# Weight-block sums loaded through a third buffer, low parts moved between DMA and VectorE, and two down slabs carried by the up stream

## The chip, the cores and the metric

The kernel runs on one NeuronCore of a Trainium2 chip. Inside a core, TensorE (PE) multiplies matrices, VectorE (DVE) and ScalarE (ACT) do elementwise work, GpSimd (POOL) and SyncE (SP) issue DMAs here. The metric is the device time of one execution in microseconds; less is better.

## The reference

One encoder layer on a sequence of 512 positions with 1024 channels, in float32. Only its last part is touched by the change, a gated feed-forward net:

```python
FFN_DIM = 3072
...
        h = rmsnorm(x, ffn_pre_norm[l])
        up = causal_dwconv(h @ w_ffn_up[l], ffn_conv_w[l], ffn_conv_b[l])
        f_gate, f_val = jnp.split(up, 2, axis=-1)
        f = (jax.nn.gelu(f_gate, approximate=True) * f_val) @ w_ffn_down[l]
        x = x + rmsnorm(f, ffn_post_norm[l])
```

Ahead of it stand a Mamba-2 mixer, a gated recurrent mixer and their merge; they take the first 480 us of the execution and are the same before and after.

## The kernel before

**Precision.** Every float32 operand is split into two parts, `hi` (the value in the matmul's reduced format) and `lo` (the rest). A product is three matmuls: hi by hi, hi by lo, lo by hi. The hi part is a copy on ACT, the lo part a subtraction `src - hi`, on DVE by `tensor_sub`, or in two places by DMA: ACT writes `-hi` into `lo` and a DMA issued from POOL with `accum_op=add` adds the source to it.

**Up stage.** The up matrix is cut into 24 pairs n = 0 to 23 of slabs, a gate slab and a value slab of 128 output channels. Pairs 0 to 3 (`PLAIN`) use the general slab stream. From n = 4 the pairs repeat as two "seven" pairs and one "eight" pair (6, 9, 12, 15, 18, 21 are eights, called plain pairs below). An eight makes its 2x2 block product in full: four stretches of 12 matmuls of 512 columns, weights a11, a12 (gate), then a21, a22 (value). A seven computes the same by seven block products of 12 matmuls of 256 columns (Strassen's scheme in Winograd's form), in the order a11, s2, s4, s3, a12, s1, and a22 as the "last product", which is issued during the next pair. The s blocks are sums of weight blocks: s1 = a21 + a22, s3 = a11 + a21, s2 = s1 + a11, s4 = s2 + a12 (the value half comes out with its sign turned, which its convolution weights `negw` undo). The matching sums of the activations, `tsum`, are made once; `h_split` splits them into `comb`.

**Where the blocks come from.** `pair_load(n)` brings the two slabs of a pair (1024 KB) into one of two slots of the tile `ring` (shown as H), issued by SP two pairs ahead. `pair_sums(n)` makes s1 and s3 by DMA: SP loads the first block (256 KB) into a buffer, then POOL adds the second block from memory with an accumulating DMA. Buffers: `place("raw", n % 2)` for s1, `2 + n % 2` for s3. s2 (line 953) and s4 (line 956) are DVE additions. `w_split(g)` splits block g of the stream, five blocks ahead of its use, into a ring of six half tiles of `whi` and `wlo`. In an eight, a11 and a12 are split in one go of 1024 columns, and so are a21 and a22; for the second of these the low part goes by DMA (line 973).

**What sets the order.** PE, ACT and, up to line 297, DVE keep the program's order. From there on DVE, and SP and POOL throughout, run in the order that a scheduler chooses at build time. Each queue is then strictly in order, so an instruction that waits holds up all behind it.

**What waits for what in a seven.** `block_product` of a12 adds to the same PSUM bank that line 1021 reads (`u2`), and the last product adds to the bank that lines 1035 and 1036 read (the sums with `u4`). So PE waits for DVE there. The pair slot is free once all its blocks are split.

**Down stage.** After pair 23 the down matrix comes as 24 slabs through the general stream. Before the change the first two are loaded in slot 1 of pair 23 and split in slot 4 of pair 23 and during the first down turn, into the tile `first` (H).

Of the kernel before, what the change touches and what calls it, by code (L numbers as in the profile page):

```python
# [8 lines left out]
F32 = mybir.dt.float32  # L9
# [5 lines left out]
P = 128  # L15
D = 1024
# [40 lines left out]
def block_kernel(ctx: ExitStack, tc, x, slabs, wgate, pc, rows, out):  # L57
# [21 lines left out]
    def big16(tag, dt):  # L79
        return big.tile([P, 8, S], dt, tag=tag, name=tag, bufs=2)  # L80
# [68 lines left out]
    def load_slab():  # L149
        i = stream["load"]  # L150
        if i < end[0]:
            raws[i] = wts.tile([P, D], F32, tag="raw", name="raw")
            nc.sync.dma_start(out=raws[i], in_=slabs[i])
            stream["load"] += 1
# [26 lines left out]
    def low_parts():  # L181
        while late:
            V.tensor_sub(*late.pop(0))  # L183
# [14 lines left out]
    def split(hi, lo, src):  # L198
        A.copy(hi, src)
        V.tensor_sub(lo, src, hi.bitcast(F32))  # L200
# [683 lines left out]
    def h_split(m):  # L884
        t = lru8(F32R).rearrange("p k (two t) -> p k two t", two=2)
        comb[m] = t[:, :, 0, :], t[:, :, 1, :]
        split(comb[m][0], comb[m][1], tsum[m])

    def plain_block(half, t):
        return tuple(h[:, half * HK:(half + 1) * HK, t] for h in h2T)  # L890
# [1 line left out]
    def block_product(out, w, b, start=False):  # L892

        for k in range(HK):
            c = slice(k * P, (k + 1) * P)
            for e, (u, v) in enumerate(((0, 0), (0, 1), (1, 0))):
# [1 line left out]
                          stop=k == HK - 1 and e == 2, skip_group_check=not start)  # L898


    seven_of = [False] * PLAIN + [i % 3 != 2 for i in range(NF - PLAIN)]
    ORDER = "a11", "s2", "s4", "s3", "a12", "s1"
    blocks = [(n, q) for n in range(PLAIN, NF)
              for q in (ORDER if seven_of[n] else ("a11", "a12", "a21", "a22"))]
    place_of = {b: i for i, b in enumerate(blocks)}
    RING = 6
    pairs = ring.rearrange("p (n i) s -> p n (i s)", n=2)
    blk, room, spare = {}, {}, []

    def drawn(n, i, h):  # L910
        return slabs[UP_SLAB + 2 * n + i, :, h * S:(h + 1) * S]

    def pair_load(n):
        if n >= NF:
            return
        raw = pairs[:, n % 2, :]
        nc.sync.dma_start(out=raw.rearrange("p (i c) -> p i c", i=2),
                          in_=slabs[UP_SLAB + 2 * n:UP_SLAB + 2 * n + 2].rearrange("i p c -> p i c"))
        blk[n] = {q: raw[:, e * S:(e + 1) * S] for e, q in enumerate(("a11", "a12", "a21", "a22"))}
        blk[n]["raw"] = raw  # L920

    def pair_sums(n):

        if n >= NF or not seven_of[n]:
            return
        b = blk[n]
        for q, one, two in (("s1", (1, 0), (1, 1)), ("s3", (0, 0), (1, 0))):
            b[q] = place("raw", n % 2 + (0 if q == "s1" else 2))
            nc.sync.dma_start(out=b[q], in_=drawn(n, *one))
            G.dma_start(out=b[q], in_=drawn(n, *two), accum_op=ALU.add)  # L930

    def place(kind, i):

        key = kind, i // 2
        if key not in room:
            room[key] = wts.tile([P, D], F32 if kind == "raw" else F32R, tag=kind, name=kind)
        return room[key][:, i % 2 * S:(i % 2 + 1) * S]

    def low(lo, src, hi):
        V.tensor_sub(lo, src, hi.bitcast(F32))  # L940

    def w_split(g):

        if g >= len(blocks):
            return
        n, q = blocks[g]
        b, i = blk[n], g % RING
        both = [place(kind, i) for kind in ("whi", "wlo")]
        b["w" + q] = both
        if seven_of[n]:  # L950
            if q == "a11":
                b["s2"] = place("raw", 4)
                V.tensor_add(b["s2"], b["s1"], b["a11"])  # L953
            elif q == "s2":
                b["s4"] = place("raw", 5)
                V.tensor_add(b["s4"], b["s2"], b["a12"])  # L956
            A.copy(both[0], b[q])
            low(both[1], b[q], both[0])
            if q == "s3":
                if not spare:  # L960
                    spare.append(work.tile([P, 2, 2, S], F32R, tag="M", name="a22", bufs=1))
                b["wa22"] = [spare[0][:, n % 2, e, :] for e in range(2)]
                A.copy(b["wa22"][0], b["a22"])
                low(b["wa22"][1], b["a22"], b["wa22"][0])
        elif q in ("a12", "a22"):
            hi, lo = (room[kind, i // 2] for kind in ("whi", "wlo"))
            src = b["raw"][:, 0:D] if q == "a12" else b["raw"][:, D:2 * D]
            A.copy(hi, src)
            if q == "a12":
                low(lo, src, hi)  # L970
            else:
                A.mul(lo, hi.bitcast(F32), -1.0)
                G.dma_start(out=lo.bitcast(F32), in_=src, accum_op=ALU.add)

    row_post2 = quad()
    mid = row_post2.rearrange("p (e t) -> p e t", e=4)
# [101 lines left out]
    for i in range(PLAIN):  # L1078
        acc = up_product()
        if i == 0:  # L1080
            for k in range(0, KT, 2):
                h_whole(k)
            pair_load(PLAIN)
        elif i == 1:
            pair_load(PLAIN + 1)
        elif i == PLAIN - 2:
            pair_sums(PLAIN)
        elif i == PLAIN - 1:
            w_split(0)
            pair_sums(PLAIN + 1)  # L1090
        gt = conv(acc, pcs[:, C_FCW + 3 * i:C_FCW + 3 * i + 3], C_FCB + i, 3)
        acc = up_product()
        if i == PLAIN - 1:
            for g in range(1, 5):
                w_split(g)
        vt = conv(acc, pcs[:, C_FCW + 3 * (NF + i):C_FCW + 3 * (NF + i) + 3], C_FCB + NF + i, 3)
        f_gate(gt)
        f_done(i, gt, vt)
        if i == PLAIN - 3:
            for m in range(4):  # L1100
                h_sum(m)
        elif i == PLAIN - 2:
            for m in (1, 2, 0, 3):
                h_split(m)
    assert stream["use"] == UP_SLAB + 2 * PLAIN

    g, old = 0, None
    for n in range(PLAIN, NF):
        for slot, _ in enumerate((seven if seven_of[n] else eight)(n, old)):
            w_split(g + 5)  # L1110
            g += 1
            if slot == 0:
                pair_load(n + 2)
            elif slot == 1:
                pair_sums(n + 2)
            if n < NF - 1:
                continue
            if slot == 1:
                for k in stream:
                    stream[k] = DOWN_SLAB  # L1120
                end[0] = slabs.shape[0]
                first = big16("H", F32R).rearrange("p (i w h) s -> p i w (h s)", i=2, w=2)
                places.update({DOWN_SLAB + e: (lambda e=e: (first[:, e, 0, :], first[:, e, 1, :]))
                               for e in range(2)})
                load_slab()
                load_slab()
            elif slot == 3:
                f_split(0)
                f_split(1)
            elif slot == 4:  # L1130
                split_slab()
                low_parts()
            elif slot == 5:
                f_split(2)
                f_split(3)
        old = n

    def down_turn(kp):
        n = NF - 1
# [93 lines left out]
```

## Time and profile before

| | us |
|---|---|
| median of 3 runs (lowest, highest) | 904.65 (904.01, 905.19) |
| the profiled execution, its time | 904.62 |
| its span, first to last instruction | 902.9 |
| PE busy in the span | 869.8 (96%) |
| DVE, ACT, POOL busy | 581.0, 438.7, 34.6 |

The profile is one execution on the one core. Its time is 1.7 us more than its span, and 0.03 us off the median. Busy PE is not PE at its peak, so the useful number is where PE stands still and where its granted clock falls.

### The profile page before, as it was taken

The numbers are of one execution on the slowest core, as the hardware profiler recorded it, in microseconds if no ns is written. First come the engines' busy times: TensorE is split into PE (matmuls) and PEld (weight loads), VectorE is DVE, ScalarE is ACT, GpSimd is POOL, SyncE is SP. The second block draws the span as 40 slices with busy tenths as digits, with TensorE's granted clock in tenths as the row PEclk, the third lists the DMA queues.
The fourth block names the chain that finished last, engine by engine and source line by source line (L and its number), as shares of the span: only waits on it lengthen the run. The fifth ranks groups of instructions, "written<-read, shape, count | busy, mean of one in ns | idle before, by whom it ended". The sixth has DMA issues, their size and how long they took to land.

```text
span 902.9 us, 11645 instructions
## 1 busy us (share of the span) xinstructions
PE 869.8 (96%) x4554; PEld 741.5 (82%) x4554; DVE 581.0 (64%) x903; ACT 438.7 (49%) x712; POOL 34.6 (4%) x52
## 2 busy tenths in 40 slices
PE   7999999999999999999999988999999989899996
PEld 5888887888778888888889977989888978788885
DVE  6777657987874453444567595867877877743225
ACT  6444536568583443222465364555555546533122
POOL 0000000000000000000000111111111100000000
PEclk9999999999999999999999999999999999999999
DMA  6232232312425322223363736567667642422312
GB/s 224 89 141 94 95 120 88 107 60 70 154 86 180 140 94 94 94 95 108 132 212 107 187 91 166 162 157 190 174 163 183 195 109 94 140 97 96 111 47 93
DMA packets 35959, 113.71 MB, mean 126 GB/s; under 512 B 3840, under 2 KB 5056, under 8 KB 35392
## 3 DMA queue, kind: packets, MB, share of 16 engines
q1 hardware_dynamic: 30432, 100.39, 32.1%
q0 software_dynamic: 5472, 12.59, 7.8%
q8 instruction: 35, 0.57, 0.3%
q14 instruction: 20, 0.16, 0.1%
HBM read 103.49 MB, written 2.13 MB: 117 GB/s over the span
## 4 chain that ended last, share of the span: by engine, by line
PE 59%; DVE 19%; DMA 10%; ACT 7%; issue 4%; SPq 0%; DVEq 0%; ACTq 0%; POOLq 0%; POOL 0%
PE ps L53 59%; DMA raw<-slabs 7%; DVE tmp L226 5%; DVE wlo L940 4%; ACT tmp L53 2%; DMA Y<-C 2%; ACT whi L53 1%; ACT L L53 1%; DVE wlo L183 1%; DVE L L644 1%; DVE raw L953 1%; DVE raw L956 1%; DMA wlo<-H 1%; DVE Y L854 1%; DVE L L200 1%
## 5 line engine op out<-in xcount | busy, mean ns | idle before, releaser
L53 PE MATMUL ps<-H,whi 128*128 128x512 f32 x720 | 225.4, 396 | 1.6 <-DVE H L53 1.6
L183 DVE TENSOR_TENSOR wlo<-raw,whi 128x1024 fp32r<-128x1024 f32 x97 | 118.4, 1222 | 121.3 <-ACT whi L53 118.9
L53 ACT CAST whi<-raw 128x1024 fp32r<-128x1024 f32 (+1 forms) x151 | 133.0, 885 | 126.5 <-PE ps L53 106.3
L53 PE MATMUL ps<-C,whi 128*128 128x256 f32 (+1 forms) x656 | 168.3, 339 | 4.1 <-DVE quad L1021 4.1
L53 PEld LDWEIGHTS ps<-H,whi 128*128 128x128 f32 x720 | 134.8, 189 | 31.4 <-issue 2.4
L53 PE MATMUL ps<-H,wlo 128*128 128x512 f32 x352 | 137.9, 392 | 0.4 <-DVE wlo L183 0.4
L53 PE MATMUL ps<-C,wlo 128*128 128x512 f32 (+1 forms) x360 | 123.6, 343 | 8.0 <-DMA wlo<-H 6.9
L53 PEld LDWEIGHTS ps<-C,whi 128*128 128x128 f32 x656 | 112.9, 191 | 17.4 <-ACT whi L53 2.9
L53 PE MATMUL ps<-L,whi 128*128 128x256 f32 (+1 forms) x400 | 87.2, 300 | 0.0
L53 PEld LDWEIGHTS ps<-C,wlo 128*128 128x128 f32 x360 | 68.8, 191 | 18.4 <-DMA wlo<-H 9.1
L226 DVE SCALAR_TENSOR_TENSOR tmp<-ps,pcs,tmp 128x511 f32<-128x511 f32 (+2 forms) x100 | 74.3, 744 | 12.6 <-ACT tmp L53 11.7
L53 PE MATMUL ps<-whi,H 128*128 128x512 f32 x256 | 81.4, 394 | 0.0
L53 PEld LDWEIGHTS ps<-H,wlo 128*128 128x128 f32 x352 | 66.4, 189 | 15.5 <-DVE wlo L183 1.2
L53 PEld LDWEIGHTS ps<-L,whi 128*128 128x128 f32 x400 | 64.4, 191 | 2.5
L53 PEld LDWEIGHTS ps<-whi,H 128*128 128x128 f32 x256 | 48.1, 188 | 10.4 <-issue 0.5
L53 ACT ACTIVATE tmp<-tmp 128x512 f32<-128x512 f32 x36 | 22.8, 632 | 61.9 <-DVE tmp L226 61.9
L53 PE MATMUL ps<-wlo,H 128*128 128x512 f32 x128 | 49.8, 389 | 0.0
L930 POOL DMA_DIRECT2D raw<-slabs x28 | 24.2, 884 | 662.4 <-DVE quad L745 468.4
L53 ACT ACTIVATE tmp<-ps,pcs 128x512 f32<-128x512 f32 x40 | 31.1, 777 | 34.3 <-PE ps L53 34.3
L53 PE MATMUL ps<-L,wlo 128*128 128x256 f32 x168 | 47.5, 283 | 0.0
L53 ACT ACTIVATE tmp<-ps,halfb 128x512 f32<-128x512 f32 x32 | 21.6, 688 | 49.6 <-PE ps L53 49.6
L940 DVE TENSOR_TENSOR wlo<-raw,whi 128x512 fp32r<-128x512 f32 x56 | 37.7, 684 | 5.4 <-ACT whi L53 5.4
(207 smaller groups left out, 1321.7 us busy)
## 6 DMA issues: line engine op xcount, KB each, us to landing
raw<-slabs SPq DMA_DIRECT2D x109, 512.0 KB, 3.2
H<-slabs SPq DMA_DIRECT2D x20, 1024.0 KB, 5.6
raw<-slabs SPq DMA_DIRECT2D x28, 256.0 KB, 3.1
raw<-slabs POOLq DMA_DIRECT2D x28, 256.0 KB, 5.3
quad<-x SPq DMA_DIRECT2D x8, 512.0 KB, 4.1
M<-acsD SPq DMA_DIRECT2D x4, 1024.0 KB, 4.6
wlo<-H POOLq DMA_DIRECT2D x6, 512.0 KB, 5.9
Y<-C SPq DMA_DIRECT2D x4, 512.0 KB, 3.9
```

The lines of the kernel that those rows point to most:

```text
L53: return lambda *args, **kw: self.tc.keep_in_program_order(op(*args, **kw))
L183: V.tensor_sub(*late.pop(0))
L200: V.tensor_sub(lo, src, hi.bitcast(F32))
L226: V.scalar_tensor_tensor(out=t[:, d:], in0=acc[:, :S - d], scalar=w[:, taps - 1 - d:taps - d], in1=t[:, d:], op0=ALU.mult, op1=ALU.add)
L644: V.tensor_tensor_scan(out=qq[:, e, :], data0=aa[:, e, :], data1=uu[:, e, :], initial=0.0, op0=ALU.mult, op1=ALU.add)
L854: V.tensor_mul(f_tile(i), gt, vt)
L930: G.dma_start(out=b[q], in_=drawn(n, *two), accum_op=ALU.add)
L940: V.tensor_sub(lo, src, hi.bitcast(F32))
L953: V.tensor_add(b["s2"], b["s1"], b["a11"])
L956: V.tensor_add(b["s4"], b["s2"], b["a12"])
```

## The change

- `pair_sums(n)` is called in slot 0 instead of slot 1, right behind `pair_load`, and it issues both first loads ahead of both adds. s1 rotates over three buffers instead of two (the third is the tile `third`, in the place of a scratch tile); s3 alternates by the count of seven pairs. The sums of pair 4 are asked for one step later in the program.
- In an eight, the low part of a21 and a22 is a DVE subtraction of 1024 columns; the ACT negation and the POOL DMA go.
- In `h_split`, the four low parts of the activation sums, DVE subtractions before, become an ACT negation and an accumulating POOL DMA each (512 KB).
- The first two down slabs ride as a 25th pair, an eight, at the end of the block stream: loaded by `pair_load(24)`, split by `w_split` in slots 2 and 4 of pair 23 into the ring of half tiles. The tile `first` goes.

```diff
@@ -884,7 +884,10 @@
-        split(comb[m][0], comb[m][1], tsum[m])
+        hi, lo = comb[m]
+        A.copy(hi, tsum[m])
+        A.mul(lo, hi.bitcast(F32), -1.0)
+        G.dma_start(out=lo.bitcast(F32), in_=tsum[m], accum_op=ALU.add)
@@ -898,20 +901,23 @@
-    seven_of = [False] * PLAIN + [i % 3 != 2 for i in range(NF - PLAIN)]
+    seven_of = [False] * PLAIN + [i % 3 != 2 for i in range(NF - PLAIN)] + [False]
...
+    turn_of = {n: i for i, n in enumerate(n for n in range(NF) if seven_of[n])}
+    third = work.tile([P, S], F32, tag="junk", name="third", bufs=1)
@@ -921,12 +927,15 @@
-        b = blk[n]
-        for q, one, two in (("s1", (1, 0), (1, 1)), ("s3", (0, 0), (1, 0))):
-            b[q] = place("raw", n % 2 + (0 if q == "s1" else 2))
+        b, i = blk[n], turn_of[n]
+        b["s1"] = third if i % 3 == 2 else place("raw", i % 3)
+        b["s3"] = place("raw", 2 + i % 2)
+        adds = ("s1", (1, 0), (1, 1)), ("s3", (0, 0), (1, 0))
+        for q, one, two in adds:
             nc.sync.dma_start(out=b[q], in_=drawn(n, *one))
+        for q, one, two in adds:
             G.dma_start(out=b[q], in_=drawn(n, *two), accum_op=ALU.add)
@@ -966,11 +975,9 @@
-            if q == "a12":
-                low(lo, src, hi)
-            else:
-                A.mul(lo, hi.bitcast(F32), -1.0)
-                G.dma_start(out=lo.bitcast(F32), in_=src, accum_op=ALU.add)
+            low(lo, src, hi)
+            if n == NF:
+                splits[DOWN_SLAB + (q == "a22")] = hi, lo
@@ -1102,38 +1107,35 @@
-            w_split(g + 5)
+            w_split(g + RING - 1)
             g += 1
             if slot == 0:
                 pair_load(n + 2)
-            elif slot == 1:
                 pair_sums(n + 2)
...
-            if slot == 1:
-                for k in stream:
-                    stream[k] = DOWN_SLAB
+            if slot == 2:
+                stream.update(load=DOWN_SLAB + 2, split=DOWN_SLAB + 2, use=DOWN_SLAB)
...
-            elif slot == 4:
-                split_slab()
-                low_parts()
```

On the DVE queue, around the first plain pair (n = 6), before, from the line that adds to `u2` of pair 5 on. L940 are low parts (the one of 1024 columns is a11 and a12 of pair 6), L995 and L226 the value half of pair 4, L953 and L956 are s2 and s4 of pair 7, L1034 to L1036 the outputs of pair 5:

```order
L1021 TENSOR_TENSOR quad<-quad,ps 128x256
L940 TENSOR_TENSOR wlo<-H,whi 128x1024
L995 TENSOR_TENSOR tmp<-quad,ps 128x256
L226 SCALAR_TENSOR_TENSOR tmp<-tmp,negw 128x511
L226 SCALAR_TENSOR_TENSOR tmp<-tmp,negw 128x510
L953 TENSOR_TENSOR raw<-raw,H 128x512
L854 TENSOR_TENSOR H<-tmp 128x512
L1034 TENSOR_TENSOR quad<-quad,ps 128x256
L940 TENSOR_TENSOR wlo<-H,whi 128x512
L1035 TENSOR_TENSOR tmp<-ps,quad 128x256
L1036 TENSOR_TENSOR tmp<-ps,quad 128x256
```

The same place now, from the same low part on (L949 was L940, L962 and L965 were L953 and L956, L1002 was L995, L1041 to L1043 were L1034 to L1036):

```order
L949 TENSOR_TENSOR wlo<-H,whi 128x1024
L962 TENSOR_TENSOR raw<-third,H 128x512
L1002 TENSOR_TENSOR tmp<-quad,ps 128x256
L965 TENSOR_TENSOR raw<-raw,H 128x512
L226 SCALAR_TENSOR_TENSOR tmp<-tmp,negw 128x511
L226 SCALAR_TENSOR_TENSOR tmp<-tmp,negw 128x510
L949 TENSOR_TENSOR wlo<-H,whi 128x1024
L854 TENSOR_TENSOR H<-tmp 128x512
L1041 TENSOR_TENSOR quad<-quad,ps 128x256
L949 TENSOR_TENSOR wlo<-H,whi 128x512
L1042 TENSOR_TENSOR tmp<-ps,quad 128x256
L1043 TENSOR_TENSOR tmp<-ps,quad 128x256
```

s2 of pair 7 reads the third buffer and stands three places earlier; s4 and the second low part of 1024 columns have come in ahead of the outputs of pair 5.

On the SP queue, from the first sums on, before. L929 are first loads of sums (raw_4132 holds both s1 buffers, raw_4135 both s3 buffers), L917 pair loads (first those of pairs 4 and 5, then 6, 7, 8), L871 the copies from which the activation sums are made:

```order
L929 DMA raw_4132<-slabs 128x512 x2
L917 DMA H_3964<-slabs 128x2x1024 x2
L871 DMA Y_3967<-C_3363 128x1024 x4
L929 DMA raw_4135<-slabs 128x512 x3
L917 DMA H_3964<-slabs 128x2x1024
L929 DMA raw_4132<-slabs 128x512
L929 DMA raw_4135<-slabs 128x512
L917 DMA H_3964<-slabs 128x2x1024
L929 DMA raw_4132<-slabs 128x512
L917 DMA H_3964<-slabs 128x2x1024
```

The same now (L937 was L929, L923 was L917; raw_4188 holds two s1 buffers, third_3968 is the third, raw_4189 holds both s3 buffers):

```order
L937 DMA raw_4188<-slabs 128x512 x2
L923 DMA H_3964<-slabs 128x2x1024 x2
L937 DMA third_3968<-slabs 128x512
L871 DMA Y_3967<-C_3363 128x1024 x4
L937 DMA raw_4189<-slabs 128x512 x3
L923 DMA H_3964<-slabs 128x2x1024
L937 DMA raw_4188<-slabs 128x512
L937 DMA raw_4189<-slabs 128x512
L923 DMA H_3964<-slabs 128x2x1024
L937 DMA raw_4188<-slabs 128x512
L923 DMA H_3964<-slabs 128x2x1024
```

The s1 of pair 7 has moved from behind the load of pair 7 to ahead of the copies; the load that stands behind the load of pair 7 is now that of pair 10.

On the ACT queue, where `h_split` stands, now (before, the four casts `L<-Y` stood together without the ACTIVATEs between them; what follows is the first block of pair 4 and the gate convolution of pair 3, as before):

```order
L53 CAST L<-Y 128x4x256
L53 ACTIVATE L<-L 128x4x256
L53 CAST L<-Y 128x4x256
L53 ACTIVATE L<-L 128x4x256
L53 CAST L<-Y 128x4x256
L53 ACTIVATE L<-L 128x4x256
L53 CAST L<-Y 128x4x256
L53 ACTIVATE L<-L 128x4x256
L53 CAST whi<-H 128x512
L53 ACTIVATE tmp<-ps,pcs 128x512
```

Four instructions more stand ahead of the first cast of pair 4.

## Rows read from the trace of the kernel before

**Rows 1.** The page, part 1: busy us (share of the span) x instructions.

```profile
PE 869.8 (96%) x4554; PEld 741.5 (82%) x4554; DVE 581.0 (64%) x903; ACT 438.7 (49%) x712; POOL 34.6 (4%) x52
```

**Rows 2.** Waits of PE, 495 to 775 us: us in total, times, longest.

```profile
PE ps L53 <- DMA wlo<-H: 6.9, 5, 2.4
PE ps L53 <- DVE quad L1021: 4.1, 5, 2.7
PE ps L53 <- DVE tmp L1036: 3.4, 1, 3.4
PE ps L53 <- DVE H L183: 2.0, 2, 1.1
PE ps L53 <- ACT H L53: 1.4, 1, 1.4
```

**Rows 3.** Timeline of PE, five places: start, us, then idle before and releaser.

```profile
533.95 0.38 PE L53 MATMUL ps<-C,wlo 128*128 128x256 f32 x1 [0.84 <-DVE wlo L940]
...
542.42 0.48 PE L53 MATMUL ps<-C,whi 128*128 128x256 f32 x2 [2.70 <-DVE quad L1021]
...
564.50 2.93 PE L53 MATMUL ps<-L,a 128*128 128x256 f32 x12 [3.42 <-DVE tmp L1036]
...
599.86 0.50 PE L53 MATMUL ps<-C,wlo 128*128 128x512 f32 x1 [0.57 <-DMA wlo<-H]
...
734.02 0.50 PE L53 MATMUL ps<-C,wlo 128*128 128x512 f32 x1 [2.40 <-DMA wlo<-H]
```

**Rows 4.** Windows: us, then busy PE, PEld, DVE, ACT, POOL, PEclk, DMA.

```profile
564.00:568.00 4.00, 3.50 (x14) 3.38 (x15) 3.06 (x6) 2.16 (x4) 0.00 (x0) 0.57 0.67 238
734.00:740.00 6.00, 5.98 (x19) 4.77 (x20) 4.45 (x9) 3.70 (x7) 0.00 (x0) 0.72 0.53 175
542.00:546.00 4.00, 3.58 (x30) 3.61 (x31) 3.81 (x8) 2.45 (x5) 0.36 (x1) 1.00 0.71 187
600.00:700.00 100.00, 95.02 (x650) 87.56 (x651) 77.38 (x133) 54.19 (x90) 12.91 (x15) 1.00 0.64 174
```

**Rows 5.** Timeline of ACT and DVE around the first plain pair.

```profile
555.01 1.06 ACT L53 ACTIVATE wlo<-whi 128x1024 fp32r<-128x1024 f32 x1
...
561.56 0.69 DVE L953 TENSOR_TENSOR raw<-raw,H 128x512 f32<-128x512 f32 x1 [5.94 <-DMA raw<-slabs]
```

**Rows 6.** Waits of DVE and of SP's queue in the up stage.

```profile
DVE raw L953 <- DMA raw<-slabs: 21.3, 6, 5.9
...
SPq L917 <- DMA wlo<-H: 81.1, 6, 14.4
```

**Rows 7.** DMA issues in 546.5:547, 502.5:503, 520:760: KB each, us to landing.

```profile
H<-slabs SPq DMA_DIRECT2D x1, 1024.0 KB, 8.0
...
Y<-C POOLq DMA_DIRECT2D x1, 512.0 KB, 9.7
...
wlo<-H POOLq DMA_DIRECT2D x6, 512.0 KB, 5.9
```

**Rows 8.** Line 917 (pair loads), all 20 of its issues.

```profile
DMA to landing us min/median/max: 4.7/5.6/8.5
```

**Rows 9.** Timeline of ACT and DVE between `h_split` and the first stall of pair 4.

```profile
524.76 3.89 ACT L53 CAST L<-Y 128x1024 fp32r<-128x1024 f32 x4
528.55 0.62 ACT L53 CAST whi<-H 128x512 fp32r<-128x512 f32 x1
...
529.81 3.49 DVE L200 TENSOR_TENSOR L<-Y,L 128x1024 fp32r<-128x1024 f32 x3
533.22 0.68 DVE L940 TENSOR_TENSOR wlo<-H,whi 128x512 fp32r<-128x512 f32 x1
...
541.87 0.41 DVE L1021 TENSOR_TENSOR quad<-quad,ps 128x256 f32<-128x256 f32 x1
```

**Rows 10.** Timeline of DVE and ACT where the first two down slabs are split.

```profile
759.67 1.22 DVE L183 TENSOR_TENSOR H<-raw,H 128x1024 fp32r<-128x1024 f32 x1
...
768.17 1.04 ACT L53 CAST H<-raw 128x1024 fp32r<-128x1024 f32 x1
```

More of the change, by code (lines that the diff above doesn't have):

```diff
@@ L898, in block_product @@
                           stop=k == HK - 1 and e == 2, skip_group_check=not start)
-    seven_of = [False] * PLAIN + [i % 3 != 2 for i in range(NF - PLAIN)]
+    seven_of = [False] * PLAIN + [i % 3 != 2 for i in range(NF - PLAIN)] + [False]
     ORDER = "a11", "s2", "s4", "s3", "a12", "s1"
-    blocks = [(n, q) for n in range(PLAIN, NF)
+    blocks = [(n, q) for n in range(PLAIN, NF + 1)
               for q in (ORDER if seven_of[n] else ("a11", "a12", "a21", "a22"))]
@@ L913, in pair_load @@
     def pair_load(n):
-        if n >= NF:
+        if n > NF:
             return
@@ L922, in pair_sums @@
     def pair_sums(n):
-        if n >= NF or not seven_of[n]:
+        if n > NF or not seven_of[n]:
             return
-        b = blk[n]
-        for q, one, two in (("s1", (1, 0), (1, 1)), ("s3", (0, 0), (1, 0))):
-            b[q] = place("raw", n % 2 + (0 if q == "s1" else 2))
+        b, i = blk[n], turn_of[n]
[3 more added lines that the diff above has]
+        for q, one, two in adds:
             nc.sync.dma_start(out=b[q], in_=drawn(n, *one))
+        for q, one, two in adds:
             G.dma_start(out=b[q], in_=drawn(n, *two), accum_op=ALU.add)
@@ L1085, in block_kernel @@
             pair_load(PLAIN + 1)
-        elif i == PLAIN - 2:
-            pair_sums(PLAIN)
         elif i == PLAIN - 1:
@@ L1104, in block_kernel @@
                 h_split(m)
+            pair_sums(PLAIN)
     assert stream["use"] == UP_SLAB + 2 * PLAIN
@@ L1117, in block_kernel @@
                 continue
-            if slot == 1:
-                for k in stream:
-                    stream[k] = DOWN_SLAB
+            if slot == 2:
+                stream.update(load=DOWN_SLAB + 2, split=DOWN_SLAB + 2, use=DOWN_SLAB)
                 end[0] = slabs.shape[0]
[L1122 to L1125, printed above, removed]
+                assert len(blocks) % RING == 4
                 load_slab()
@@ L1136, in block_kernel @@
         old = n
+    for kind in ("whi", "wlo"):
+        for _ in range(2):
+            wts.tile([P, D], F32R, tag=kind, name=kind)
     def down_turn(kp):
```

## The prediction

> **What bounds the kernel now.** I read the page first: PE is busy 96% of the span [rows 1], so the most that a change of order can give is the time in which PE stands still or runs at a low clock. The list of PE's waits says where that is. Nearly all of it lies in the up stage and at the border to the down stage: 17.8 us in five rows [rows 2], and 0.84 us in pair 4 [rows 3]. Next I went to these places in the timeline and asked what was late.
>
> - 6.9 us in five waits: the second low part of a plain pair, made by ACT and a POOL DMA, isn't there when PE wants a21. The longest is 2.40 us [rows 3].
> - 3.4 us once: in pair 6 PE wants to add the last product of pair 5 to a bank that DVE has not yet read (line 1036). DVE was late because it stood 5.94 us at line 953 (s2 of pair 7), waiting for the DMA that adds up s1 [rows 5]. DVE waited so six times, 21.3 us together [rows 6]; the other five cost PE little, as DVE had slack there.
> - 4.1 us in five waits for line 1021: 2.70 us of it in pair 4 [rows 3], the other four together 1.4 us.
> - 3.4 us in three waits for parts of the first two down slabs (lines 183 and the ACT cast into H) [rows 2].
> - The 0.84 us are for the first low part of pair 4.
>
> Then the clock. Over 564 to 568 us its mean is 0.57, so 4 x 0.43 = 1.7 us of work are lost; over 734 to 740 it is 0.72, and 6 x 0.28 = 1.7 us are lost [rows 4]. Half of full speed is 1.2 of 2.4 GHz. Both falls follow a standstill, of 3.42 and 2.40 us. The 2.70 us in pair 4 were followed by no fall: 542 to 546 shows 1.00 [rows 4]. So 3.4 us more hang on two of the waits.
>
> **The change part by part.** *Sums a pair sooner.* s1 of the first seven behind a plain pair used the buffer that the seven just ahead of the plain pair still held, so its load, its add and s2 stood in one chain. With the third buffer the load stands one pair load earlier in SP's queue (for pair 7 even ahead of the activation copies). The sums are then there long before DVE wants them, and the 21.3 us of DVE waiting [rows 6] lose their cause. What is late next is the other input of s2: a11 of the same pair, from the pair load. Pair 7's load was issued at 546.6 and landed after 8.0 us [rows 7], the slowest but little of all (4.7 to 8.5, median 5.6) [rows 8]: at 554.6, or 555.0 with the 0.4 us of delay that I derive below. The new DVE order puts s2 there, ahead of the outputs of pair 5. From s2 to L1043 it is eleven instructions; DVE's mean in 600 to 700 us is 77.38/133 = 0.58 us each [rows 4], so 6.4 us, and L1043 ends at 561.4. PE reached that point at 564.50 - 3.42 = 561.1 [rows 3], now 561.5. So the 3.42 us shrink to between 0 and 0.5; I take 0.4, since a wait for a semaphore comes on top. Gain 3.0 us, and the 1.7 us of low clock behind it.
>
> *Low part of a plain pair on DVE.* Removed: six ACT negations of 1.06 us [rows 5] and six 512 KB DMAs that take 5.9 us to land [rows 7]. Added: six DVE subtractions of 1024 columns, 1.22 us each by the same form at the border [rows 10]. The low part then follows its hi part by some 1.2 us and what DVE has queued, instead of 7, and is done five instructions ahead of L1043, which PE needs first. So the 6.9 us go, and 1.7 us of low clock at 734. Their cover is DVE's free time: it is busy 77.4 of 100 us in the stage [rows 4]; three pairs take 33.5 us there (the same wait at 599.86 and 734.02, four times three pairs apart [rows 3]), 25.9 of them DVE's, and one subtraction more, with PE's standstills gone, makes 27.1 us of some 31.5, that is 86%. Without that cover they would cost at most 6 x 1.22 = 7.3 us. A second effect: SP no longer waits for these DMAs before the next pair load, which it did for 81.1 us, six times [rows 6], so the loads behind plain pairs start earlier.
>
> *The four small waits at line 1021* (1.4 us) come one slot after DVE has made s2 and s4 of the following pair. In the new order both are made some ten instructions earlier, during the plain pair, so line 1028 stands about 1.2 us earlier in the queue against waits of 0.3 us. I count 1.4 us gained, bounds 0 and 1.4.
>
> *The low parts of the activation sums by DMA.* This is the part that gives nothing. It takes four subtractions off DVE (three take 3.49 us [rows 9]) and puts four negations on ACT, which is in order and has its first cast of pair 4 right behind. Four pairs of copy and dependent negation take about 4 x 2.0 = 8.1 us instead of 3.9 (1.06 us for a negation [rows 5], 0.97 for a copy [rows 9]), so that cast moves from 528.55 to 532.9 and DVE's low part from 533.22 [rows 9] to 533.55. All that DVE does from there to line 1021 (541.87) is the same list in the same order. So the 2.70 and the 0.84 us stay, and the stage begins 0.4 us later (bounds: 0.2 less, 1.0 more). The DMAs are on no path as far as I see: the first can start at about 527, and 512 KB take 5.9 us alone and 9.7 with others in flight [rows 7], so 533 to 537. PE does a block in 1.44 us (four in the 5.77 us between 533.95 and 542.42 less 2.70 [rows 3]), wants the first of them at 535.6, and would stand until 542.8 anyway; the others follow 2 us apart and are wanted 3 or more us apart.
>
> *Down slabs in the block stream.* The low part of the first ended at 760.9 and the hi part of the second at 769.2 [rows 10], just behind PE. Now they are split in slots 2 and 4 of pair 23, some 7 and 3 us ahead of the first down turn, in ring places that PE has just left. All 3.4 us of waits go; DVE's subtractions are the same in number. Bounds 2.0 and 3.4, as DVE now stands at L1041 of pair 23 ahead of the second one, which PE wants 5 us later.
>
> **The sum**, against the profiled time of 904.62 (the median of the runs, 904.65, is the same for this purpose): 6.9 + 3.0 + 1.4 + 3.4 + 3.4 (clock) - 0.4 = 17.7 us, so **887.0**.
>
> **The rivals.**
> - *Pair loads take the place of the sums (slower).* s2 now stands ahead of the outputs that PE waits for, and s2 needs the pair load. At pair 6 that load may take 561.5 - 6.4 - 547.0 = 8.1 us before PE stands; order and buffers are alike at the other five plain pairs. Each us beyond costs six, and with a fall of the clock at each, 1.7 more. Slower than before it is from (17.7 - 10.2)/6 = 1.25 us beyond, a landing of 9.4 us each time; at 10 us it would be 887.0 + 6 x (1.9 + 1.7) = 908.6. Against it: the longest of twenty took 8.5, the median 5.6 [rows 8], and 3 MB of DMA leave the stage for 2 MB that come in ahead of it. 4%.
> - *DVE paces the sevens.* With 86% of DVE used, the small waits at line 1021 stay and a like one appears in the other sevens, 0.3 us in each of 14: 887.0 + 4.2 = 891.2, or 890 where only half of them do. For it: a seven holds 19 DVE instructions, 11.0 us by the mean above, and its seven blocks take PE 10.1. Against it: a plain pair has seven, some 5 us with its two long ones, for 48 matmuls of 512 columns, so DVE catches up there. 20%.
> - *The sums aren't sooner in effect*, since POOL's adds stand behind the four activation DMAs and SP's loads behind pair loads. Then the stall in pair 6 stays with its clock, and the small waits: 887.0 + 3.0 + 1.7 + 1.4 = 893.1. The order of SP's queue speaks against it. 7%.
> - *No change.* The four activation DMAs run one behind the other at 9.7 us each [rows 7], landing at 537, 546, 556 and 566. PE then stands about 5, 7 and 2.5 us beyond what it stands now, with one or two falls of the clock: 887.0 + 14.5 + 2.6 = 904.1. The rows of the copies show them overlapping, three us apart. 2%.
> - *The front gains too*, because DVE comes to pair 4 with less behind it: without the 3.5 us and the 0.4 it is 883.1. 6%.
> - *The clock falls in pair 4*, where some 2.8 us of standstill remain: 887.0 + 1.7 = 888.7. By the rows, 2.40 and 3.42 us dropped the clock and 2.70 didn't, so length alone doesn't decide. 25% of what follows for the forecast, and inside its range. The Trainium skill (TensorE: Matmul & The Clock Gate, Part 1: The HAM clock gate) says that the gate's window runs freely and isn't set by the kernel's start; by that rule a standstill of this size can drop the clock in one execution and not in another, and the time would be the 888.7 just given. The trace agrees in that the shorter of two gaps was the one that dropped the clock.
>
> **How the numbers follow.** The forecast, waits gone but for pair 4, gets 61%, with its own range 885.0 to 889.5 (0.5 us on terms unknown, the clock in pair 4 above). The range for 8 in 10 reaches into the case of the pacing DVE and up to the sums that are not sooner, and down to the front that gains: 883.0 to 893.0, which leaves out the two cases at 904 and beyond, and half of the 7%. A measurement of this kernel tells 0.2%, 1.8 us, from no change. All cases but two are faster by more: 0.93; the case of no change and half a percent of others 0.03; slower 0.04.
>
> **What would show it.** In the profile after: no wait of PE for a DMA into wlo; DVE's wait for s1 gone, and at s2 of pair 7 one of about 2 us for the pair load; PE's wait for L1043 in pair 6 under 0.5 us; waits for L1028 only in pair 4, still 2.7 to 3.1 us; the granted clock at 1.00 from pair 5 to the tail; no wait between pair 23 and the second down turn; ACT's first cast of pair 4 about 4 us later. Wrong I would be by a new wait for a pair load in front of every plain pair, or by low parts of the activation sums that land later than PE's standstill covers.

## The result, and the profile after

The changed kernel took 894.91 us (median of 4 runs, 894.21 to 899.18), the kernel before 904.92 beside it (4 runs, 904.01 to 907.18). The ratio is 0.9896, with a 95% interval of 0.986 to 0.9931: 9.4 us faster, between 6.2 and 12.7. The prediction had 17.7 us and 887.0. The sign was right, the size was not: the time lies 1.9 us above the upper end of the range. Ratios, here and below, leave out runs more than 1.5% above the fastest of the same kernel.

Part 1 of the page after, which answers to [rows 1]: PE works as long as before, in a span that is shorter (893.4 us, before 902.9).

```profile
PE 868.6 (97%) x4554; PEld 742.6 (83%) x4554; DVE 583.4 (65%) x905; ACT 435.0 (49%) x710; POOL 34.5 (4%) x50
```

The waits of PE from 480 to 775 us, which answer to [rows 2]: us in total, times, longest.

```profile
PE ps L53 <- DMA L<-Y: 6.0, 2, 4.6
PE ps L53 <- DVE quad L1028: 1.7, 2, 1.1
PE ps L53 <- DVE tmp L1043: 1.4, 1, 1.4
PE ps L53 <- DVE wlo L183: 1.2, 1, 1.2
PE ps L53 <- ACT whi L53: 0.7, 1, 0.7
PE ps L53 <- DVE wlo L949: 0.2, 1, 0.2
```

The waits for a DMA into wlo (6.9 us) and those for the down slabs (2.0 and 1.4 us) are gone. Line 1028 is the old 1021, line 1043 the old 1036. The first row is new and is the largest: PE waits for L, the low part of an activation sum. L<-Y is the accumulating DMA of `h_split`, which the prediction had on no path.

The timeline of PE shows where that is, in pairs 4 and 5; the last row is pair 6.

```profile
540.38 0.39 PE L53 MATMUL ps<-L,whi 128*128 128x256 f32 x1 [1.41 <-DMA L<-Y]
543.07 0.77 PE L53 MATMUL ps<-C,whi 128*128 128x256 f32 x2 [1.11 <-DVE quad L1028]
550.82 0.58 PE L53 MATMUL ps<-L,whi 128*128 128x256 f32 x1 [4.63 <-DMA L<-Y]
571.82 1.70 PE L53 MATMUL ps<-L,a 128*128 128x256 f32 x12 [1.43 <-DVE tmp L1043]
```

Now the engine that issues these DMAs. The timeline of POOL, the four adds of `h_split` (line 890), with the idle time before each:

```profile
527.57 1.30 POOL L890 DMA_DIRECT2D L<-Y  x1 [0.29 <-issue]
535.15 1.28 POOL L890 DMA_DIRECT2D L<-Y  x1 [6.28 <-ACT whi L53]
540.70 1.28 POOL L890 DMA_DIRECT2D L<-Y  x1 [4.27 <-issue]
551.15 1.28 POOL L890 DMA_DIRECT2D L<-Y  x1 [9.16 <-issue]
```

And the DMA issues of four windows, each holding one of these adds: KB, us from issue to landing.

```profile
L<-Y POOLq DMA_DIRECT2D x1, 512.0 KB, 7.2
...
L<-Y POOLq DMA_DIRECT2D x1, 512.0 KB, 5.2
...
L<-Y POOLq DMA_DIRECT2D x1, 512.0 KB, 10.1
...
L<-Y POOLq DMA_DIRECT2D x1, 512.0 KB, 5.3
```

Put the two together: 527.57 + 7.2 = 534.8, and the second add is issued at 535.15. 535.15 + 5.2 = 540.35, and the third goes at 540.70. 540.70 + 10.1 = 550.8, and the fourth goes at 551.15. Each add is issued some 0.35 us after the one before it has landed, though ACT had made its input long ago (its last copy and negation end at 533.2). The releaser named at the second add is ACT, but it had finished that work earlier; the two with "issue" show no semaphore at all. So the four land at 534.8, 540.3, 550.8 and 556.4.

The clock falls there too. Windows of after: us, busy PE, PEld, DVE, ACT, POOL, PEclk, DMA.

```profile
542.00:544.00 2.00, 0.93 (x4) 0.96 (x5) 2.00 (x4) 0.46 (x2) 0.00 (x0) 0.69 1.14 307
544.00:546.00 2.00, 2.00 (x11) 1.89 (x9) 1.84 (x4) 1.29 (x3) 0.00 (x0) 0.50 0.79 178
546.00:548.00 2.00, 0.18 (x1) 0.00 (x0) 0.18 (x1) 0.89 (x2) 0.00 (x0) 0.96 1.19 209
...
550.00:552.00 2.00, 1.19 (x5) 1.19 (x6) 0.00 (x0) 0.00 (x0) 0.85 (x2) 0.50 0.04 12
552.00:554.00 2.00, 2.00 (x12) 2.00 (x11) 0.43 (x2) 0.00 (x0) 2.00 (x4) 0.50 0.58 93
554.00:556.00 2.00, 2.00 (x11) 2.00 (x11) 1.39 (x4) 0.98 (x2) 1.11 (x2) 0.50 1.23 184
556.00:558.00 2.00, 2.00 (x17) 2.00 (x17) 1.88 (x3) 0.58 (x2) 0.00 (x0) 0.90 1.20 160
...
600.00:700.00 100.00, 99.98 (x683) 93.01 (x683) 84.54 (x142) 52.89 (x91) 10.33 (x13) 1.00 0.61 171
```

There are two falls, one behind the waits of 1.41 and 1.11 us and one behind the wait of 4.63 us; between them the mean is 0.96. PE's busy time at half clock (1.2 GHz) is 0.93 + 2.00 us in the first fall (PE starts again at 543.07; the 0.69 takes in its standstill before that) and 1.19 + 2.00 + 2.00 us in the second. It loses half of itself, 4.1 us, and 0.2 more in the window from 556 us: 4.3 us in all. The last row is what the change was good for: between 600 and 700 us PE stands still for 0.02 us, where it stood 5 us before [rows 4].

Pair 6 has a knock-on. Three adds of `pair_sums` had queued on POOL behind the fourth activation add, were issued one right behind the other from 551.90 on, and ran beside the load of pair 7. DVE in pair 6, and the DMAs that were being issued between 554.5 and 554.8 us:

```profile
564.99 0.69 DVE L962 TENSOR_TENSOR raw<-third,H 128x512 f32<-128x512 f32 x1 [4.12 <-DMA H<-slabs]
```

```profile
H<-slabs SPq DMA_DIRECT2D x1, 1024.0 KB, 10.3
raw<-slabs POOLq DMA_DIRECT2D x1, 256.0 KB, 12.1
```

A pair load of 10.3 us instead of 8.0 [rows 7] holds s2 of pair 7, and PE waits 1.43 us for line 1043 where 0 to 0.5 were predicted. That the adds beside it made the load slow is likely, but no run tests it alone; in the versions below whose activation adds overlap, this load took 5.4 to 7.3 us.

### The profile page after: what moved, and what is told of

Read it like the earlier page. It is cut to its first block, busy times and chain, and to the rows that moved or that the text cites. A ratio compares the mean times of both kernels' runs of the same rounds, so it can differ in the third digit from the quotient of the medians.

```text
span 893.4 us, 11607 instructions
## 1 busy us (share of the span) xinstructions
PE 868.6 (97%) x4554; PEld 742.6 (83%) x4554; DVE 583.4 (65%) x905; ACT 435.0 (49%) x710; POOL 34.5 (4%) x50
## 4 chain that ended last, share of the span: by engine, by line
PE 67%; DVE 13%; DMA 9%; ACT 5%; issue 4%; POOL 0%; SPq 0%; DVEq 0%; POOLq 0%; ACTq 0%
PE ps L53 67%; DMA H<-slabs 5%; DVE tmp L226 3%; DVE wlo L949 2%; DMA Y<-C 2%; DVE wlo L183 1%; ACT whi L53 1%; DMA L<-Y 1%; ACT tmp L53 1%; ACT L L53 1%; DVE L L644 1%; DMA raw<-slabs 1%; DVE raw L962 1%; DVE tmp L662 0%; DVE L L638 0%
## 5 line engine op out<-in xcount | busy, mean ns | idle before, releaser
L53 ACT CAST whi<-raw 128x1024 fp32r<-128x1024 f32 (+1 forms) x147 | 130.0, 891 | 102.9 <-PE ps L53 98.0
L53 PE MATMUL ps<-L,whi 128*128 128x256 f32 (+1 forms) x400 | 89.1, 304 | 6.0 <-DMA L<-Y 6.0
L226 DVE SCALAR_TENSOR_TENSOR tmp<-ps,pcs,tmp 128x511 f32<-128x511 f32 (+2 forms) x100 | 74.3, 744 | 11.2 <-ACT tmp L53 10.3
L53 PEld LDWEIGHTS ps<-whi,H 128*128 128x128 f32 x256 | 48.1, 188 | 10.4 <-issue 0.5
L949 DVE TENSOR_TENSOR wlo<-H,whi 128x512 fp32r<-128x512 f32 (+1 forms) x42 | 36.2, 862 | 14.2 <-ACT whi L53 14.1
L939 POOL DMA_DIRECT2D raw<-slabs x24 | 21.4, 1014 | 612.4 <-DVE quad L745 467.1
```

The costliest lines, as they stand in the source:

```text
L53: return lambda *args, **kw: self.tc.keep_in_program_order(op(*args, **kw))
L226: V.scalar_tensor_tensor(out=t[:, d:], in0=acc[:, :S - d], scalar=w[:, taps - 1 - d:taps - d], in1=t[:, d:], op0=ALU.mult, op1=ALU.add)
```

## Experiments

The theory: the terms for the plain pairs, the sums and the down slabs stand, and the activation low parts, priced at nothing, cost about 8 us, since POOL issues an add of 512 pieces of 1 KB (128 rows of four, as hi and lo alternate in the tile) only when the one before has landed. The main rival: the other terms were smaller than predicted.

**Low parts of the activation sums back on DVE, the rest as changed.**

```diff
-        A.copy(hi, tsum[m])
-        A.mul(lo, hi.bitcast(F32), -1.0)
-        G.dma_start(out=lo.bitcast(F32), in_=tsum[m], accum_op=ALU.add)
+        split(hi, lo, tsum[m])
```

> The changed kernel with one edit undone: the low parts of the four activation sums are DVE subtractions again. Theory (the accumulating DMAs of these low parts run one behind the other and PE waits 6.0 us for two of them, loses some 4 us of clock and 1.4 us more at pair 6): these go and the time is the predicted sum without its 0.4 us, 885.5 to 887.5 us. Rival (the stall comes from the front's DMA load as a whole or from DVE, and shifts elsewhere): 891 us or more.

Measured: 890.37 us (887.01 to 891.98), ratio 0.9837 (0.9811 to 0.9863), 14.7 us faster than before. So the other three parts are worth that without this one, and by the medians this one takes some 5 us of it away. The median lay between what the two sides had written; a second measurement is below. PE's list has no wait for L, but 2.2 us for line 1041 in pair 6, as the load of pair 7 took 9.7 us here.

**The same DMA, with hi and lo apart.** The tile holds hi in its first 4 KB of a row and lo in the second, so that an add has 128 pieces of 4 KB. The order of instructions on every engine is that of the changed kernel.

```diff
-        t = lru8(F32R).rearrange("p k (two t) -> p k two t", two=2)
-        comb[m] = t[:, :, 0, :], t[:, :, 1, :]
+        t = lru8(F32R).rearrange("p k s -> p (k s)")
+        comb[m] = tuple(t[:, e * D:(e + 1) * D].rearrange("p (k t) -> p k t", k=HK) for e in range(2))
```

> The changed kernel with the low parts still made by DMA, but hi and lo of a sum each 4 KB in one piece per partition, so that one add has 128 rows of 4 KB and not 512 pieces of 1 KB; the order on every engine is the same. Theory (what holds the next add back is the room for descriptors, which 512 pieces fill): adds issued 2 us apart as ACT delivers them, no wait of PE for L<-Y, 886 to 888 us. Rival 1 (the adds are slow because they move 512 KB within the chip beside the weight loads): issues may come closer, but PE still waits 4 us or more, 892 to 895 us. Rival 2 (POOL simply runs one add at a time): issue gaps as before, 893 to 895 us.

Measured: 888.74 us (886.22 to 891.42), ratio 0.9824 (0.9799 to 0.9849), 0.7 us above the 886 to 888 of the theory. POOL's timeline of the four adds:

```profile
529.26 0.86 POOL L890 DMA_DIRECT2D L<-Y  x1 [0.17 <-issue]
531.30 0.85 POOL L890 DMA_DIRECT2D L<-Y  x1 [1.17 <-ACT L L53]
533.33 0.86 POOL L890 DMA_DIRECT2D L<-Y  x1 [1.18 <-ACT L L53]
535.36 0.84 POOL L890 DMA_DIRECT2D L<-Y  x1 [1.18 <-ACT L L53]
```

Now they go 2 us apart, as fast as ACT makes their inputs, and overlap. PE doesn't wait for L at all. This is what the prediction had assumed.

**The same with half the room.** `dynamic_dma_scratch_size` sets the size of a scratch room for POOL's DMAs; the theory is that each piece takes a place in it until its DMA has landed. Here the room is halved.

```diff
-    dynamic_dma_scratch_size=2048
+    dynamic_dma_scratch_size=1024
```

> As the kernel with contiguous low parts, but with half the scratch room for POOL's DMA descriptors (1024 for 2048). Theory (descriptor room is what serialises adds): now adds of 128 pieces are held back too; the four copies' adds at 500 us and the four low parts are issued only when the former has landed, 5 us or more apart, and the time is 3 us or more above that of the full room. Rival (room plays no part): within 1 us of it, and issues as close.

Measured: 888.09 us in one run, so the time expected of it, 3 us above the full room, did not come. But the timeline of POOL shows the mechanism:

```profile
500.79 0.89 POOL L872 DMA_DIRECT2D Y<-C  x1 [5.21 <-DMA Y<-C]
501.99 0.86 POOL L872 DMA_DIRECT2D Y<-C  x1 [0.32 <-issue]
503.38 0.86 POOL L872 DMA_DIRECT2D Y<-C  x1 [0.53 <-issue]
506.83 0.84 POOL L872 DMA_DIRECT2D Y<-C  x1 [2.60 <-issue]
```

The first of these adds landed after 5.8 us, at 506.6, and the fourth was issued 0.25 us later; with the whole room it goes 0.55 us after the third is done. The second, third and fourth of the activation adds show the same: each goes 0.30 to 0.31 us behind the landing that brings the pieces in flight down to 256. So half the room holds three adds of 128 pieces (384) and not four (512). By that the whole room holds 768 and not 1024 pieces: one add of 512 at a time, which is the changed kernel. Waits of 1 to 3 us on POOL cost no time that this one run shows.

**Adds in halves.** With that I could foretell a third case: three adds of 256 pieces fit, a fourth doesn't.

```diff
-        G.dma_start(out=lo.bitcast(F32), in_=tsum[m], accum_op=ALU.add)
+        for k in range(0, HK, HK // 2):
+            G.dma_start(out=lo[:, k:k + HK // 2].bitcast(F32), in_=tsum[m][:, k:k + HK // 2],
+                        accum_op=ALU.add)
```

> The changed kernel with each add into an activation low part issued as two of 256 pieces instead of one of 512 (same pieces of 1 KB, same bytes). With half the room for descriptors three adds of 128 pieces were in flight and the fourth was issued 0.2 to 0.3 us after the first had landed, so the whole room holds 768 pieces but not 1024. By that three halves are in flight at a time, the parts land some 4 us apart instead of 5 to 10, PE's waits for L<-Y fall from 6.0 us to 0 to 2 and the time to 888 to 891 us. Rival: it is the short pieces into every other KB of a row that make adds follow one another, not their count; then each half is issued when the one before has landed, the waits stay near 6 us and the time at 893 to 897.

Measured: 886.93 us (886.42 to 887.75), ratio 0.9782 (0.9751 to 0.9812). POOL's timeline of the eight halves:

```profile
528.56 3.62 POOL L891 DMA_DIRECT2D L<-Y  x3 [0.27 <-issue]
534.47 3.81 POOL L891 DMA_DIRECT2D L<-Y  x3 [2.29 <-PE ps L53]
538.54 2.46 POOL L891 DMA_DIRECT2D L<-Y  x2 [0.25 <-issue]
```

Three go before any has landed; the first takes 5.7 us and lands at 534.2, and at 534.47 the next goes. Each of the other four also goes 0.31 to 0.34 us behind a landing. The pieces are as short as in the changed kernel and lie in every other KB as there, so it isn't their length that lines the adds up, but their number. PE's wait for L<-Y falls from 6.0 us to nothing, and 8.0 us come back by the medians for a change of one statement, 6.6 in the second measurement below. The theory had 888 to 891 us, a little too much.

**Activation low parts by DMA alone**, on the kernel before.

```diff
-        split(comb[m][0], comb[m][1], tsum[m])
+        hi, lo = comb[m]
+        A.copy(hi, tsum[m])
+        A.mul(lo, hi.bitcast(F32), -1.0)
+        G.dma_start(out=lo.bitcast(F32), in_=tsum[m], accum_op=ALU.add)
```

> The kernel before with only the activation sums' low parts made by ACT and POOL adds. Theory (POOL issues an add of 512 pieces of 1 KB only when the one before has landed, so the four land 5 to 10 us apart): PE waits some 6 us more in pairs 4 and 5, with 2 to 4 us of low clock behind it, 8 to 10 us slower than before, 1.009 to 1.011. By the prediction's step (adds overlap, nothing of it on the path) it would be 0.4 us slower, 1.0005.

Measured: 1.007 of before (1.0039 to 1.0102), 6.3 us slower, between 3.5 and 9.2; the theory had 8 to 10, the prediction's step 0.4. The timeline of PE:

```profile
538.98 0.39 PE L53 MATMUL ps<-L,whi 128*128 128x256 f32 x1 [0.93 <-DMA L<-Y]
...
547.71 0.58 PE L53 MATMUL ps<-L,whi 128*128 128x256 f32 x1 [3.78 <-DMA L<-Y]
```

The same two waits, with none of the change's other parts present, and again each add goes 0.35 to 0.38 us behind the landing of the one before.

**The third buffer alone**, on the kernel before: `turn_of`, `third`, both loads ahead of the adds, `pair_sums` in slot 0.

```diff
-            b[q] = place("raw", n % 2 + (0 if q == "s1" else 2))
+        b["s1"] = third if i % 3 == 2 else place("raw", i % 3)
+        b["s3"] = place("raw", 2 + i % 2)
...
-            elif slot == 1:
                 pair_sums(n + 2)
```

> The kernel before with the third buffer and the earlier sums alone. Theory (the sum of the prediction by terms): the stall in pair 6 (3.0), its clock (1.7) and the small waits at line 1021 (1.4) go, 6.1 us: 898 to 900 us; the waits for wlo<-H stay at 6 to 8 us. Rival (the plain pair's DMA sits in the same POOL queue and pair load chain, so nothing is gained without the other edit): 902 us or more.

Measured: 896.44 us (895.03 to 899.9), ratio 0.9915 (0.9886 to 0.9945), 7.7 us faster, between 5.0 and 10.3: the 6.1 expected lie inside. The waits for wlo<-H fell with it, from 6.9 to 4.6 us, and the longest from 2.4 to 1.3 us, which nothing in the prediction said. The other profiles point the same way: these waits are 6.1 us in the version just above and 9.1 in the one with the down slabs alone, both with two buffers, and 4.8 in the later one with three.

**The plain pairs' low parts alone**, on the kernel before.

```diff
-            if q == "a12":
-                low(lo, src, hi)
-            else:
-                A.mul(lo, hi.bitcast(F32), -1.0)
-                G.dma_start(out=lo.bitcast(F32), in_=src, accum_op=ALU.add)
+            low(lo, src, hi)
```

> The kernel before with only the second low part of a plain pair moved from ACT and a POOL DMA to DVE. The prediction's term for it was 6.9 us of waits for wlo<-H and 1.7 us of low clock behind the longest of them: 8.6 us faster than before, 0.9905 of its time. If the six subtractions that DVE takes on pace it instead, waits for lines 1021 and 1036 grow and no more than 4 us remain (0.9955 or more). The stall in pair 6 stays in either case.

Measured: 1.0068 of before (1.0031 to 1.0106), 6.2 us slower, where 8.6 us faster was expected. The ratio counts five of ten runs; all ten spread from 905.0 to 927.6 us, with a median of 918.4, so 6.2 us is the least of it. The waits for wlo<-H are gone as foretold, and PE's list has this instead (line 1032 is the old 1036):

```profile
PE ps L53 <- DVE tmp L1032: 19.2, 6, 4.4
```

The timeline of DVE, SP, POOL and PE at one of the six places:

```profile
649.72 0.69 DVE L940 TENSOR_TENSOR wlo<-raw,whi 128x512 fp32r<-128x512 f32 x1
650.43 0.33 SPq L929 DMA_DIRECT2D raw<-slabs  x1
...
658.24 0.87 POOL L930 DMA_DIRECT2D raw<-slabs  x1 [8.80 <-DMA raw<-slabs]
...
664.51 0.69 DVE L953 TENSOR_TENSOR raw<-raw,H 128x512 f32<-128x512 f32 x1 [5.70 <-DMA raw<-slabs]
...
665.92 2.75 PE L53 MATMUL ps<-L,a 128*128 128x256 f32 x12 [4.19 <-DVE tmp L1032]
```

Read it as a chain: DVE splits s1 of one seven, its buffer is free at 650.4, SP loads the first block of the next s1 into it at once, POOL adds the second when the load has landed, and DVE gets the sum after 14.1 us, just ahead of the output that PE waits for. This chain was there before at all six plain pairs, and PE's standstill at the low part of the pair gave it time. Take that away without the buffer, and PE meets the chain itself, with another subtraction of 1.22 us on DVE: DVE's waits for these sums are 28.5 us where they were 21.3 [rows 6]. The four longest of PE's six waits, 3.9 to 4.4 us, are each followed by a fall of the clock that costs 1.7 us.

**The down slabs alone**, on the kernel before.

```diff
-    blocks = [(n, q) for n in range(PLAIN, NF)
+    blocks = [(n, q) for n in range(PLAIN, NF + 1)
...
+            if n == NF:
+                splits[DOWN_SLAB + (q == "a22")] = hi, lo
```

> The kernel before with only the first two down slabs in the block stream (the second low part of that last pair by ACT and DMA, as in the other plain pairs). The prediction's term: 3.4 us of waits at the border go, 0.9962 of the time before. If the low part by DMA, which takes some 7 us behind its hi part, comes too late for the down stage, a new wait for a DMA into wlo of 1 to 3 us takes its place there and the time is that of before, 0.998 to 1.001.

Measured: 0.9938 of before (0.991 to 0.9966), 5.6 us faster, between 3.1 and 8.2: the 3.4 predicted lie inside. The waits for H at the border are gone from PE's list. The list also shows wlo<-H at 9.1 us in six waits instead of 6.9 in five. The sixth, 0.91 us, stands at the border: it is the late low part that the expectation named, only smaller. One of the others is 3.94 us long and has 3.0 us of low clock around it; the profiled execution was the longest of its eight (905.04, the others 897.8 to 901.1), so what that wait is worth in the others stays open.

**Third buffer and down slabs, without either change of low parts.** And, on the same chip, the first and the best of the versions above once more.

```diff
-            low(lo, src, hi)
+            if q == "a12":
+                low(lo, src, hi)
+            else:
+                A.mul(lo, hi.bitcast(F32), -1.0)
+                G.dma_start(out=lo.bitcast(F32), in_=src, accum_op=ALU.add)
```

(against the version with the sums' low parts on DVE)

> The third buffer and the down slabs of the change, with the second low part of a plain pair as before (ACT negation and POOL add) and the activation low parts as before (DVE). The prediction's step on the low parts: with the sums sooner the waits for wlo<-H are 4.6 us in the kernel that has the third buffer alone, and one fall of the clock stands behind them, so this is 4.6 to 6.5 us slower than the same kernel with the low parts on DVE (e12_e1_again): 0.989 to 0.991 of before. Rival: the six subtractions cost PE what they take of DVE, as they did where they were moved alone (6 us slower than before); then this is as fast as the other or faster by some us, 0.980 to 0.985.

> e1_sums_on_dve once more, on the same chip as its counterpart: 0.9837 of the time before, 0.981 to 0.986. No theory expects another.

> e9_adds_in_halves once more beside it: 0.978 to 0.983 of the time before. If overlapping DMAs for the activation low parts are worth what they free of DVE, it is 0 to 3 us faster than e12_e1_again; if that part of the change gives nothing, as the prediction had it (0.4 us slower), the two are the same within 2 us.

Measured: 892.18 us (890.54 to 893.68), ratio 0.9857 (0.9831 to 0.9884), for the two parts; 888.37 (886.36 to 891.9), 0.982 (0.9788 to 0.9851), with the plain pairs' low parts on DVE as well; 888.31 (885.14 to 890.25), 0.9822 (0.9794 to 0.985), with the activation adds in halves on top. The first was expected at 0.989 to 0.991. So in company of the third buffer the low parts on DVE give some 3.8 us by the medians, where alone they cost 6.2 or more; the runs of the two versions just overlap (890.5 to 893.7 and 886.4 to 891.9), so the size is rough. The waits of PE show the same, of the first and of the second:

```profile
PE ps L53 <- DMA wlo<-H: 4.8, 4, 1.5
```

```profile
PE ps L53 <- DVE tmp L1041: 2.8, 3, 1.3
```

4.8 us go and 2.3 come at line 1041, up from 0.5. And the activation part, once its adds overlap, gives nothing that these runs can tell: 0.06 us between the medians, with four runs of each spread over some 5 us. Its first measurement, 886.93, was 1.4 us lower, within that spread. In the profiles it does take something away: the 2.8 us at line 1041, 1.3 of them in pair 6, are 0.3 us with the halves.

## Why the prediction was wrong

- **The step that failed** is the one on the low parts of the activation sums: the first add "can start at about 527, and 512 KB take 5.9 us alone and 9.7 with others in flight [rows 7], so 533 to 537", and "the others follow 2 us apart". The first half held (527.57, landing at 534.8). The second did not: they landed 5.6, 10.4 and 5.6 us apart. It is what the prediction itself had named as a sign of being wrong: low parts "that land later than PE's standstill covers". The row that I leaned on, the adds Y<-C [rows 7], overlapped because each has 128 pieces; the adds into L have 512, and two don't fit. All runs agree on the limit: 128-piece adds overlap, 256-piece adds go three at a time, 512-piece adds one at a time. A larger room wasn't tried; so that the room is what holds them rests on the halved one, where three adds of 128 pieces went and a fourth waited.
- **What it cost**: the ratios of the versions whose adds overlap (0.9824, 0.9782, 0.9822) are 0.007 to 0.011 under that of the changed kernel, 6.5 to 10.3 us. In the profiles: 6.0 us of waits for L, the 1.4 us in pair 6, where the versions whose adds overlap don't stand, and 4.3 us of low clock instead of their 1.7, less 1.7 us by which the wait at line 1028 in pair 4 got shorter (1.1 instead of 2.8), as PE came there later: 6.0 + 1.4 + 2.6 - 1.7 = 8.3 us.
- **The rival "no change"** had this mechanism and 2%. It took 9.7 us for each add, so landings at 537, 546, 556 and 566 and 904.1 us; the measured ones are 534.8, 540.3, 550.8 and 556.4. The sentence that set it aside, that the rows of the copies show them overlapping, compared DMAs of the same bytes and not of the same number of pieces. The Trainium skill (DMA: Bandwidth & Descriptors, Terms, and SWDGE vs HWDGE vs iDMA) says that software on GpSimd writes the descriptors of its DMAs into rings in SBUF. The Trainium skill (the same page, Why a DMA increments its semaphore by 16 and not by 1) says, where it speaks of DMAs from SP and ACT, that one descriptor moves one contiguous run. The traces agree in that it is the count of runs that decides, 512 against 128; where the room lies no run here shows.
- **The sum of the rest** was near: with overlapping adds the time is 888.7, 886.9 and 888.3 us against 887.0. That is luck in part, since its terms missed in both directions, as the points below show. In each of these profiles the clock fell behind the 2.8 us in pair 4, which the prediction had as a rival with 888.7. The windows from 542 to 548 us of the version with the third buffer alone and of the one measured at 888.37:

```profile
542.00:548.00 6.00, 4.00 (x33) 4.03 (x34) 5.81 (x11) 3.07 (x6) 1.14 (x2) 1.00 0.79 246
```

```profile
542.00:548.00 6.00, 5.73 (x35) 5.76 (x36) 4.31 (x9) 2.55 (x5) 0.85 (x1) 0.72 0.67 173
```

The same standstill, 2.69 us in both, was followed by full clock (2.4 GHz) in the one and by a fall of 6 x 0.28 = 1.7 us of work in the other.

- **Right within a few tenths**: waits for wlo<-H and for the down slabs gone, the two falls of the clock at 564 and 734 us with them, the first cast of pair 4 at 533.15 (532.9 predicted), and DVE idle until it.
- **Right in the number for another reason**: pair 6. The 0.4 us rested on a load of pair 7 of 8.0 us, with s2 waiting for it. In the four profiles whose adds overlap the load took 5.4 to 7.3 us, and PE doesn't stand in pair 6. With the sums' low parts on DVE it took 9.7 and 8.8 us, and PE stood 2.2 and 1.3 us. What sets this load's time stays open.
- **Right in the sum, wrong as separate terms**: the 6.9 us for the plain pairs' low parts and the 3.0 + 1.4 for the sums. The third buffer alone gave 7.7 and took 2.3 us of the former; the low parts gave some 3.8 behind it and cost 6.2 or more without it. "The other five cost PE little, as DVE had slack there" was wrong in its reason: the 19.2 us above say that the slack was PE's own wait.
- **Small misses**: the prediction took 1.8 us as what a measurement can tell from no change; the interval above reaches 3.3 us to either side. The stage begins later by more than the 0.4 us: PE waits 1.0 to 1.2 us for line 183 at about 522 us in every version with the third buffer (0.2 to 0.5 without it). DVE there waits 6.5 to 6.9 us for the DMAs Y<-C instead of 4.4 to 4.7; I didn't test whether the earlier sums delay these. The four small waits at line 1021 went, but one of 0.6 to 1.5 us came between 600 and 710 us in the changed kernel and in three of the four profiles whose adds overlap.

## What to carry to other kernels

Price a DMA by its pieces as well as by its bytes: look in the layout how many contiguous runs it has, and take a row with the same count for its overlap. When several adds from POOL follow one another at once, read their issues beside the landings; an issue that always comes some 0.3 us behind a landing, with no semaphore named, was waiting for room in these runs. And waits on one cyclic path aren't separate terms: a standstill that is removed gives only as much as the next one on the same cycle leaves, so ask which other chain had been finishing unseen during that standstill.

## What I had not expected of the hardware

- POOL holds back an accumulating DMA until enough earlier ones have landed: at a scratch size of 2048, three of 256 pieces or one of 512 go; at 1024, three of 128. Behind one of 512 three of 128 still went (551.90 us in the changed kernel, before the landing at 556.4), so the limit at 2048 lies between 896 and 1024 pieces. The issue follows the landing by 0.25 to 0.4 us, and the instruction shows as "issue" or under an engine that had long been done.
- In the changed kernel an add of 512 KB in 512 pieces landed in 5.2 to 7.2 us, and once in 10.1 us; in 128 pieces, four overlapping took 8.0 to 9.2 us. Most took longer each, but the four were done at 544.6 instead of 556.4 us.
- A standstill of 2.69 us dropped the clock in one kernel and not in another, and one of 2.40 us did before [rows 3, 4].
